# V by class and the dilated partial sums go through DRAM; one swap of the K halves for both sample granules

## Chip, cores and metric

One core of one Trainium2 chip runs the kernel. The metric is device time in microseconds (us), the median over executions; lower is better. The engines are PE (matrix products; PEld is its weight load), DVE and ACT (element-wise and row work), POOL (the same, slower), and SP, which in this kernel does nothing but issue every DMA, in one queue, in the order of the program.

## The reference, cut to what matters

Two encoder layers run over a prompt of 512 rows and a sample of 1024 rows, model width 1024. Layer 0 has grouped-query attention and differential attention, layer 1 has a dilated one, with 16 heads of 64. Only layer 1 is touched by two of the three edits:

```python
C_PATTERNS = ((128, 1), (512, 4), (2048, 16))       # (window, dilation)
def odd_layer(x, norm_g, w_in, w_out, c_q_norm, c_k_norm):
    z = rms_norm(x, norm_g) @ w_in
    q, k, v, gate = jnp.split(z, _split_points(ODD_SPLITS), axis=-1)
    q = partial_rope(rms_norm(q.reshape(B, S, C_HEADS, HEAD_DIM), c_q_norm))
    k = partial_rope(rms_norm(k.reshape(B, S, C_HEADS, HEAD_DIM), c_k_norm))
    o = dilated_attention(q, k, v).reshape(B, S, C_W)
    return x + (o * jax.nn.silu(gate)) @ w_out
def dilated_attention(q, k, v):                      # for each pattern: attention within a
    for window, dilation in C_PATTERNS:              # band, over the rows of one class
        o, lse = dilated_branch(q, k, v, window, dilation)   # (row modulo the dilation)
    w = jax.nn.softmax(jnp.stack(lses, axis=0), axis=0)      # the three are merged by their
    return jnp.sum(w[..., None] * jnp.stack(outs, axis=0), axis=0)   # softmax denominators
```

## The kernel before

**Tiling.** The rows are three granules of 512: granule 0 is the prompt, 1 and 2 are the halves of the sample. Each layer is cut into eight units; in layer 1 (kind "C") a unit is two heads, 128 columns. For each unit and granule there is a projection of K and V, one of Q and the gate, and the attention; at a layer's end come the output projection and the residual.

**K and q.** `qk_stages` normalises and rotates K or q into `st`, which a DMA transpose turns (L594: `K<-st`, `q<-st`). K is needed with its two halves of 64 partitions also the other way round: two DMAs, L599 and L600 (`K<-K`, 64 partitions each), make that swapped copy, for each of the three granules.

**V and the classes of four.** V is in `u.V`, 128 rows by 128-row tile. Pattern 1 uses it as it is. Patterns 2 and 3 are computed together ("p23") over rows of one class modulo four, and need V as `Vc`, where partition p holds rows 4p to 4p+3. Before the change `Vc<-V` (L682) copies each 128-row tile from SBUF to SBUF in a DMA of its own: four per granule.

**An attention batch** is a chain over four engines and a DMA: PE makes the scores `S` (L1122 for p23, L1170 and L1175 for pattern 1), DVE masks and takes the row maximum (L1097), ACT makes the exponential (L1107), ACT rounds to f16 (`h`, L796), DVE subtracts to get the low half (`h`, L800), SP issues a DMA transpose (`t<-h`, L359), and PE multiplies by V ("AV", L784).

**The send.** The p23 sums lie by class; pattern 1's lie by row. ACT packs the p23 sums and denominators into `pk`, and four DMAs (`pn<-pk`, L1152) bring them to row order in `pn`. The merge of the patterns reads `pn`, and its result `sg` is spilled to DRAM (`mixbuf<-sg`, L816). At the end of the layer it comes back (`f<-mixbuf`, L1269), is split and transposed, and goes through the output projection on PE (L492, operands `whl` and `t`).

**What sets the order.** Every piece is a stage with assumed costs (`dve()`, `act()`, `pe()`, and for a DMA an issue on SP plus a time and a tail) that a list-scheduling planner places; instructions are emitted in the planned order. The order of each engine is thus fixed when the program is built, and an engine that waits holds all that stands behind it. The planner also keeps tokens for buffers (`pnt` for `pn`, `vct` for `Vc`). Weights are loaded in f32 (`f<-in_w`, L415), squared on ACT (L423) for their norms (L432, L433 and L435 on PE), and split in two f16 halves (L473, L478).

Of the kernel before, what the change touches and what calls it, by code (L numbers as in the profile page):

```python
# [10 lines left out]
F32 = mybir.dt.float32  # L11
F16 = mybir.dt.float16
# [21 lines left out]
GI = [[0], [1, 2]]  # L34
# [179 lines left out]
def trunk_kernel(ctx: ExitStack, tc: tile.TileContext, A: dict, outs: list):  # L214
# [299 lines left out]
        return r  # L514


    def qk_stages(zb, ztok, evs, e2, tabs, tdep, ti, kind, isq, dst, dst_acq, dst_use, swap, dst_dep=()):

        b = {}
        t1t, stt_ = Token("t1"), Token("st")  # L520
# [75 lines left out]
        s = P.tdma(1024, f_T, [s, dst_dep], dst_acq, tuple(x for x in dst_use if x not in dst_acq) + (stt_,))  # L596
        if swap is None:
            return [s]
        w1 = dma(ISSUE, 0.25, lambda: nc.sync.dma_start(out=swap()[0:64], in_=dst()[64:128]), [s], (), dst_use)  # L599
        w2 = dma(ISSUE, 0.25, lambda: nc.sync.dma_start(out=swap()[64:128], in_=dst()[0:64]), [s], (), dst_use)  # L600
        return [s, w1, w2]


    class Unit:
        def __init__(self):
            self.q, self.sg, self.q_ready, self.sg_ready = {}, {}, {}, {}
            self.qtok, self.sgtok = {}, {}
            self.k_ready, self.v_ready, self.vc_ready = {}, {}, {}
            self.att_done = {}
            self.Vc = [None, None]  # L610

    last_mm = [None]
    proj_mm = {}
# [10 lines left out]
    def kv_piece(u, gi):  # L624
        g, t0, row = GRAN[gi]
        zb = {}
        ztok = Token("z")
        evs, vls = [], []
        for hf in range(2):
            pt = Token("pj")  # L630
            pb = {}
            mms = []
            for j in range(2):
                tl = t0 + 2 * hf + j

# [12 lines left out]
                proj_mm[u.l, g] = m  # L648
                mms.append(m)

            def f_ev(hf=hf, pb=pb):
                if "z" not in zb:
                    zb["z"] = new(ztok)
                S_.activation(out=zb["z"][:, :, 2 * hf:2 * hf + 2, :].rearrange("p h t d -> p t h d"),
                              in_=pb["ps"][:, :, 0:128].rearrange("p t (h d) -> p t h d", h=2), func=AF.Copy)
            evs.append(add("ACT", act(256), f_ev, mms, (), [pt, ztok], pos=P.pos - PB))
            r = row // 128 + 2 * hf

            def f_vh(r=r, pb=pb):
                if not hasattr(u, "V"):  # L660
                    u.V = new(u.vtok)
                S_.activation(out=u.V[:, r:r + 2, 0, :], in_=pb["ps"][:, :, 128:256], func=AF.Copy, scale=2.0 ** -15)
            first = (gi, hf) == (0, 0)
            vh = add("ACT", act(256), f_vh, [mms, None if first else u.v_open], [u.vtok] if first else (),
                     [pt] if first else [pt, u.vtok], pos=P.pos - PB)
            if first:
                u.v_open = vh

            def f_vl(r=r, pb=pb):
                stt(out=u.V[:, r:r + 2, 1, :], in0=pb["ps"][:, :, 128:256], scalar=2.0 ** -15,  # L670
                    in1=u.V[:, r:r + 2, 0, :], op0=M, op1=SU)
            vl = add("DVE", dve(256), f_vl, [vh], (), [pt, u.vtok], pos=P.pos - PB)
            vls.append(vl)
            if u.kind == "C":
                for j in range(2):
                    tl = t0 + 2 * hf + j

                    def f_vc(tl=tl, r=r, j=j):
                        if u.Vc[g] is None:
                            u.Vc[g] = lpool[0].tile([128, g + 1, 4, 256], F16, tag=f"Vc{g + 1}{u.vct[g].slot}", name=f"Vc{g + 1}", bufs=1)  # L680
                        p0 = 32 * (tl % 4)
                        nc.sync.dma_start(out=u.Vc[g][p0:p0 + 32, tl // 4, :, :],  # L682
                                          in_=u.V[:, r + j, :, :].rearrange("p a f -> p (a f)"))
                    if tl == 0:
                        u.vc_open = add("NONE", 0.0, None, [vl, u.tdep], [u.vct[g]])
                    vc = dma(ISSUE, 0.25, f_vc, [vl, u.vc_open], (), [u.vct[g], u.vtok])
                    u.vc_ready.setdefault(g, []).append(vc)
        u.v_ready[gi] = vls
        def kdst():
            if not hasattr(u, "K"):  # L690
                u.K = new(u.ktok)
            return u.K[:, 0, gi]
        u.k_ready[gi] = qk_stages(zb, ztok, evs, lambda: u.kvw.e2, lambda: u.ktab, u.tdep, t0, u.kind, False,
                                  kdst, [u.ktok] if gi == 0 else (), [u.ktok], lambda: u.K[:, 1, gi],
                                  () if gi == 0 else u.k_ready[0][0])
        if gi == 2:
            w_done(u.kvw, mms)

    def qg_piece(u, gi):
# [57 lines left out]
        def qdst():  # L757
            if gi not in u.q:
# [1 line left out]
            return u.q[gi]  # L760
        ti = row // 128 if u.kind == "C" else t0
        u.q_ready[gi] = qk_stages(zb, ztok, evs, lambda: u.qgw.e2, lambda: u.qtab, u.tdep, ti, u.kind, True,
                                  qdst, (), [qt], None)
        if gi == 2:
            w_done(u.qgw, mms)

# [299 lines left out]
    def att_C(u, gi):  # L1066
# [46 lines left out]
        def p23(hs):  # L1113
            def build():
                blocks = [(h, c) for h in hs for c in range(4)]

                def mm(s):
                    for i, (h, c) in enumerate(blocks):
                        q = u.q[gi][:, h, :].rearrange("p (r c) -> p c r", c=4)[:, c, :]
                        for sk in range(2):  # L1120
                            k = u.K[:, sk, GI[g][0]:GI[g][-1] + 1, h, :].rearrange("p g (t c) -> p c g t", c=4)[:, c]
                            T.matmul(s[:, L * i:L * i + L], q, k, start=(sk == 0), stop=(sk == 1))  # L1122

                def mxs(x):
                    if "md" not in ob:
                        ob["md"] = small(16, "md", 4).rearrange("p (c f) -> p c f", c=4)
                    h, c = x
                    return ob["md"][:, :, h] if c is None else ob["md"][:, c, h:h + 1]

                def avf(t4):  # L1130
                    if "o23" not in ob:
                        ob["o23"] = new(ot23).rearrange("p a b -> p (a b)").rearrange("p (c h d) -> p c h d", c=4, h=2)
                    for i, (h, c) in enumerate(blocks):
                        av(ob["o23"][:, c, h, :], t4, i * L // 128, L // 128,
                           lambda k, b: u.Vc[g][:, k, c, 128 * b + 64 * h:128 * b + 64 * h + 64])
                batch(mm, len(blocks) * pe(2 * L, 2), blocks, L, lambda x: u.m23[g][:, t0 // 4, :], mxs,
                      lambda x: ob["md"][:, x[1], 2 + x[0]:3 + x[0]], avf, [u.vc_ready[g]], avs23, ot23)
            return build

        def send():  # L1140
            def f_ev():
                ob["pk"] = lpool[0].tile([128, 4, 132], F32, tag=f"pk{pkt.slot}", name="pk", bufs=1)
                S_.activation(out=ob["pk"][:, :, 128:132], in_=ob["md"], func=AF.Copy)
                S_.activation(out=ob["pk"][:, :, 0:128], in_=ob["o23"].rearrange("p c h d -> p c (h d)"), func=AF.Copy)
            s = add("ACT", act(512) + 0.12, f_ev, avs23[-1:], [pkt], [ot23])
            s = add("NONE", 0.0, None, [s], [pnt])
            ob["sent"] = []
            for j in range(4):
                def f(j=j):
                    if j == 0:  # L1150
                        ob["pn"] = lpool[0].tile([128, 4, 132], F32, tag=f"pn{pnt.slot}", name="pn", bufs=1)
                    nc.sync.dma_start(out=ob["pn"][:, j, :],  # L1152
                                      in_=ob["pk"][32 * j:32 * j + 32, :, :].rearrange("p c f -> p (c f)"))
                ob["sent"].append(dma(ISSUE, 0.25, f, [s], (), [pkt, pnt]))
            if gi == 0 or gi == 2:
                close(u.vct[g], avs23)

# [559 lines left out]
```

## Time and profile before

| what | value |
|---|---|
| median of 3 runs | 1854.68 us (1853.79 to 1855.3) |
| profiled execution: time, span | 1854.62 us, 1852.4 us |
| mean granted clock of PE | 0.959 of full speed |
| busy share of the span: PE, PEld, DVE, ACT, POOL | 90%, 75%, 72%, 65%, 38% |
| busy share of the 16 DMA engines, main queue | 73.4% |

The span is the traced part of the profiled execution; 2.2 us of its time lie around it. The busy share of an engine is over the whole span, and an engine that is 90% busy can still stand still in single places. The program opens with layer 0 (to about 800 us), opens layer 1 (to 1000 us), runs the units of layer 1 (to about 1665 us), and ends with the last unit's batches and the output projection.

### The profile page before, as it was taken

What the parts mean: (1) busy time and instruction counts of PE and PEld (TensorE: products, weight loads), DVE (VectorE), ACT (ScalarE), POOL (GpSimd) and SP (SyncE); (2) the same over time, 40 slices, a digit from 0 to 9 for tenths busy, and PEclk for the clock granted to TensorE, in tenths of its full rate; (3) what the DMA queues carried; (4) which work ended last, traced back from release to release, by engine and by line L of the source; (5) the groups of instructions that cost most, each with busy time, mean ns of one, the idle gap of its engine ahead of it and who ended that gap; (6) DMA issues with size and microseconds to landing.
All of it is one profiled execution on the core that took longest, in us unless ns stands there. A gap on an engine that the chain in (4) does not pass through costs nothing. (4 is left out here: it accounts for less than half of the span.)

```text
span 1852.4 us, 44798 instructions
## 1 busy us (share of the span) xinstructions
PE 1675.0 (90%) x17626; PEld 1398.4 (75%) x17626; DVE 1332.2 (72%) x2985; ACT 1212.8 (65%) x2593; POOL 695.5 (38%) x1204
## 2 busy tenths in 40 slices
PE   4898978989999999699898999999999999995898
PEld 3776756878887878378787887888788888774788
DVE  7788878767888778965635778677777777787332
ACT  6488978767777767853425676678676757777220
POOL 6523333333463445312212344354444444452200
PEclk9999999999999999799899999999999999996999
DMA  9989999795565445689975676676766757776983
GB/s 251 191 157 166 182 177 167 146 163 113 98 125 101 109 92 122 147 198 224 207 176 128 122 150 131 138 143 140 147 132 144 137 116 151 148 145 140 232 230 103
DMA packets 788724, 282.06 MB, mean 152 GB/s; under 512 B 647072, under 2 KB 772256, under 8 KB 788512
## 3 DMA queue, kind: packets, MB, share of 16 engines
q1 hardware_dynamic: 788512, 279.19, 73.4%
q8 instruction: 138, 2.26, 0.5%
q14 instruction: 74, 0.61, 0.1%
HBM read 73.92 MB, written 25.17 MB: 53 GB/s over the span
## 5 line engine op out<-in xcount | busy, mean ns | idle before, releaser
L492 PE MATMUL pj<-whl,hT 128*128 128x256 f16 x7680 | 882.3, 275 | 22.2 <-DMA hT<-h 21.2
L492 PEld LDWEIGHTS <-hT 128*128 128x128 f16 x7968 | 782.8, 99 | 145.6 <-DMA hT<-h 23.1
L784 PEld LDWEIGHTS <-t 128*128 128x128 f16 x4992 | 200.5, 100 | 93.8 <-DMA t<-h 85.8
L1107 ACT ACTIVATE f<-f,cs,csc 128x256 f32<-128x256 f32 (+1 forms) x384 | 218.4, 570 | 65.5 <-DVE cs L778 65.4
L492 PEld LDWEIGHTS <-t 128*128 128x128 f16 x2304 | 228.9, 100 | 40.0 <-DMA t<-h 9.8
L800 DVE TENSOR_TENSOR h<-f,h 128x1024 f16<-128x1024 f32 x148 | 187.7, 1273 | 57.4 <-ACT h L796 55.0
L784 PE MATMUL pj<-V,t 128*128 128x64 f16 (+1 forms) x4032 | 178.7, 204 | 51.2 <-DMA t<-h 47.8
L492 PE MATMUL pj<-whl,t 128*128 128x256 f16 x1728 | 202.4, 279 | 8.2 <-DMA t<-h 8.2
L772 PE MATMUL S<-K,q 128*128 128x512 f16 x640 | 169.6, 399 | 33.3 <-ACT f L1024 19.1
L796 ACT ACTIVATE h<-f 128x1024 f16<-128x1024 f32 x168 | 175.5, 1051 | 21.9 <-DMA t<-h 19.8
L535 POOL TENSOR_SCALAR qs<-qs,we 128x8 f32<-128x8 f32 x87 | 44.5, 511 | 354.0 <-DVE qs L529 343.1
L261 POOL TENSOR_TENSOR qs<-qs,mhalf 128x8 f32<-128x8 f32 x87 | 147.8, 1699 | 7.3
L772 PEld LDWEIGHTS <-q 128*128 128x128 f16 x640 | 61.0, 101 | 91.7 <-issue 42.8
L854 DVE TENSOR_REDUCE as<-S 128x1 f32<-128x1024 f32 (+1 forms) x80 | 95.9, 1219 | 29.1 <-PE S L772 28.9
L423 ACT ACTIVATE t<-f 128x1024 bf16<-128x1024 f32 x74 | 77.8, 1051 | 44.5 <-DMA f<-in_w_in_dram 32.6
L864 ACT ACTIVATE f<-S,as,asc 128x1024 f32<-128x1024 f32 (+1 forms) x96 | 101.7, 1061 | 4.0 <-DVE h L800 0.5
L478 DVE SCALAR_TENSOR_TENSOR whl<-f,wsm,whl 128x1024 f16<-128x1024 f32 x68 | 87.7, 1305 | 8.2 <-ACT whl L473 8.2
L1332 DVE SCALAR_TENSOR_TENSOR f<-pj,os,f 128x256 f32<-128x256 f32 x96 | 41.9, 479 | 68.0 <-PE pj L492 61.2
L1018 DVE TENSOR_REDUCE bs<-S 128x1 f32<-128x1024 f32 x64 | 77.2, 1217 | 16.2 <-PE S L772 16.2
L800 POOL TENSOR_TENSOR h<-f,h 128x1024 f16<-128x1024 f32 x20 | 43.5, 2175 | 120.9 <-ACT h L796 120.9
L473 ACT ACTIVATE whl<-f,wsm 128x1024 f16<-128x1024 f32 x68 | 75.8, 1140 | 16.8 <-PE pj L492 14.3
L1122 PE MATMUL S<-K,q 128*128 128x256 f16 (+1 forms) x384 | 79.3, 371 | 4.6 <-DVE m L1097 4.6
(250 smaller groups left out, 2684.5 us busy)
## 6 DMA issues: line engine op xcount, KB each, us to landing
f<-in_w_in_dram SPq DMA_DIRECT2D x58, 512.0 KB, 5.3
mixbuf<-sg SPq DMA_DIRECT2D x48, 256.0 KB, 2.8
f<-mixbuf SPq DMA_DIRECT2D x24, 512.0 KB, 5.7
K<-K SPq DMA_DIRECT2D x78, 128.0 KB, 2.5
f<-in_w_out_dram SPq DMA_DIRECT2D x16, 512.0 KB, 4.5
pn<-pk SPq DMA_DIRECT2D x96, 66.0 KB, 2.2
x1buf<-f SPq DMA_DIRECT2D x12, 512.0 KB, 4.1
Vc<-V SPq DMA_DIRECT2D x96, 64.0 KB, 2.3
```

The lines of the kernel that those rows point to most:

```text
L261: G.tensor_tensor(y, v, mhalf[:, 0:n], ALU.pow)
L423: S_.activation(out=junk1(t1t), in_=b[i].rearrange("p k n -> p (k n)"), func=AF.Square, accum_out=b["s"][:, i:i + 1])
L478: stt(out=part(k, 1, i), in0=b[i][:, nk * k:nk * k + nk, :], scalar=sc(), in1=part(k, 0, i), op0=M, op1=SU)
L492: T.matmul(ps, lhs(k, a), wt(k, b), start=(k == 0 and i == 0), stop=(k == 7 and i == 2))
L772: T.matmul(out[:, 512 * i:512 * i + 512], q, u.K[:, st, gi, hk, :], start=(st == 0), stop=(st == 1))
L784: T.matmul(o, t4[:, 8 * a + base + k, :], v(k, b), start=(k == 0 and i == 0), stop=(k == nk - 1 and i == 2))
L796: S_.activation(out=b["hl"][:, 0, :], in_=b["e"], func=AF.Copy)
L800: (G if on_pool else V).tensor_tensor(b["hl"][:, 1, :], b["e"], b["hl"][:, 0, :], SU)
L854: V.tensor_reduce(out=b["s"][:, 0:nh], in_=b["S"].rearrange("p (h k) -> p h k", h=nh), op=ALU.max, axis=AX.X)
L864: S_.activation(out=b["e"][:, w * i:w * i + w], in_=b["S"][:, w * i:w * i + w], func=AF.Exp, bias=b["s"][:, 2 + i:3 + i], scale=u.sc, accu ...
L1107: S_.activation(out=b["e"][:, w * i:w * i + w], in_=b["e"][:, w * i:w * i + w], func=AF.Exp, bias=b["s"][:, i:i + 1], scale=u.sc, accum_ou ...
L1122: T.matmul(s[:, L * i:L * i + L], q, k, start=(sk == 0), stop=(sk == 1))
```

## The change

Three edits, and the costs that the planner assumes for the DMAs concerned:

- V goes to a DRAM tile `vd` in one DMA per granule of 256 KB (L676) and comes back from there as `Vc` in one of 256 KB (L683). `Vc` is now a tile per granule instead of one per group.
- `pk` goes to a DRAM tile `pd` in one DMA of 264 KB (L1158), and comes back in row order as `pn` in another (L1163).
- The K halves are swapped once for the prompt, and once for both sample granules after the second one's transpose (L700), in both layers. Granule 1 issues no swap of its own.

```diff
@@ qk_stages
         if swap is None:
             return [s]
-        w1 = dma(ISSUE, 0.25, lambda: nc.sync.dma_start(out=swap()[0:64], in_=dst()[64:128]), [s], (), dst_use)
-        w2 = dma(ISSUE, 0.25, lambda: nc.sync.dma_start(out=swap()[64:128], in_=dst()[0:64]), [s], (), dst_use)
-        return [s, w1, w2]
+        return [s] + swap(s)
@@ kv_piece
-            if u.kind == "C":
-                for j in range(2):
-                    tl = t0 + 2 * hf + j
...
-                        p0 = 32 * (tl % 4)
-                        nc.sync.dma_start(out=u.Vc[g][p0:p0 + 32, tl // 4, :, :],
-                                          in_=u.V[:, r + j, :, :].rearrange("p a f -> p (a f)"))
...
-                    vc = dma(ISSUE, 0.25, f_vc, [vl, u.vc_open], (), [u.vct[g], u.vtok])
-                    u.vc_ready.setdefault(g, []).append(vc)
+        if u.kind == "C":
...
+            vd = dr.tile([512, 256], F16, name=f"vd{box['n']}")
+            vs = dma(ISSUE, 0.5, lambda: nc.sync.dma_start(
+                out=vd.rearrange("(t p) f -> p t f", p=128),
+                in_=u.V[:, row // 128:row // 128 + 4].rearrange("p t a f -> p t (a f)")), [vls], (), [u.vtok])
...
+                nc.sync.dma_start(out=u.Vc[gi], in_=vd.rearrange("(p c) f -> p c f", c=4))
...
+            vc = dma(ISSUE, 0.5, f_vc, [vs, u.vc_open], (), [u.vct[g]])
+            u.vc_ready.setdefault(g, []).append(vc)
...
+        def swap(s):
...
+            for a, b in ((0, 64), (64, 0)):
+                def f_w(a=a, b=b):
+                    x = slice(GI[g][0], GI[g][-1] + 1)
+                    nc.sync.dma_start(out=u.K[a:a + 64, 1, x], in_=u.K[b:b + 64, 0, x])
+                r.append(dma(ISSUE, 0.25 + 0.2 * g, f_w, [s, u.k_ready.get(1)], (), [u.ktok]))
+            return r
         u.k_ready[gi] = qk_stages(zb, ztok, evs, lambda: u.kvw.e2, lambda: u.ktab, u.tdep, t0, u.kind, False,
-                                  kdst, [u.ktok] if gi == 0 else (), [u.ktok], lambda: u.K[:, 1, gi],
+                                  kdst, [u.ktok] if gi == 0 else (), [u.ktok], swap if gi != 1 else None,
@@ send
-            s = add("NONE", 0.0, None, [s], [pnt])
-            ob["sent"] = []
-            for j in range(4):
...
-                    nc.sync.dma_start(out=ob["pn"][:, j, :],
-                                      in_=ob["pk"][32 * j:32 * j + 32, :, :].rearrange("p c f -> p (c f)"))
-                ob["sent"].append(dma(ISSUE, 0.25, f, [s], (), [pkt, pnt]))
+            pd = dr.tile([512, 132], F32, name=f"pd{box['n']}")
+            s = dma(ISSUE, 0.5, lambda: nc.sync.dma_start(out=pd.rearrange("(p c) f -> p c f", c=4), in_=ob["pk"]),
+                    [s], (), [pkt])
...
+                nc.sync.dma_start(out=ob["pn"], in_=pd.rearrange("(j p) f -> p j f", p=128))
+            ob["sent"] = [dma(ISSUE, 0.6, f, [s], [pnt])]
```

The changed costs and stages also move the order. The programs' SP queues differ from layer 0 on, PE's order from the end of layer 0. All later lines of the file stand ten lines further down (L784 is L794, L816 is L826, L1122 is L1132, L1269 is L1279). No instruction of PE, DVE, ACT or POOL is added or removed.

The first place is SP's queue in an ordinary unit of layer 1, before (the numbers behind a tile's name count tiles):

```order
L816 DMA mixbuf_72<-sg_15020 128x4x128
L359 DMA_TRANSPOSE t_16778<-h_16745 128x16x128
L359 DMA_TRANSPOSE t_16820<-h_16780 128x16x128
L682 DMA Vc_16887<-V_15813 32x4x256 x4
L594 DMA_TRANSPOSE q_16942<-st_16817 128x8x128
L1152 DMA pn<-pk 128x1x132 x4
L682 DMA Vc_16887<-V_15813 32x4x256 x4
L359 DMA_TRANSPOSE t_17063<-h_16986 128x16x128
L594 DMA_TRANSPOSE K_16068<-st_17052 128x8x128
```

The same place of the changed program:

```order
L359 DMA_TRANSPOSE t_16793<-h_16754 128x16x128
L594 DMA_TRANSPOSE q_16826<-st_16795 128x8x128
L359 DMA_TRANSPOSE t_16831<-h_16797 128x16x128
L683 DMA Vc_16874<-vd_96 128x1024
L826 DMA mixbuf_72<-sg_15020 128x4x128
L676 DMA vd_98<-V_15825 128x4x256
L1158 DMA pd_97<-pk 128x528
L683 DMA Vc_16979<-vd_98 128x1024
L1163 DMA pn<-pd_97 128x4x132
L359 DMA_TRANSPOSE t_17068<-h_16996 128x16x128
L594 DMA_TRANSPOSE K_16082<-st_17057 128x8x128
```

Twelve plain DMAs stood between two `t` transposes; now six stand there, of which two read what another one has just written, with one DMA between the write and the read (`vd_98`, `pd_97`).

The second place is SP's queue at the end of the units, in the last unit, before:

```order
L359 DMA_TRANSPOSE t_24868<-h_24808 128x16x128
L682 DMA Vc_24928<-V_23414 32x4x256 x8
L816 DMA mixbuf_72<-sg_23462 128x4x128
L1152 DMA pn<-pk 128x1x132 x4
L359 DMA_TRANSPOSE t_25002<-h_24902 128x16x128
L594 DMA_TRANSPOSE q_25014<-st_24988 128x8x128
```

The same place of the changed program:

```order
L359 DMA_TRANSPOSE t_24821<-h_24749 128x16x128
L683 DMA Vc_24879<-vd_127 128x1024
L683 DMA Vc_24885<-vd_129 128x1024
L594 DMA_TRANSPOSE q_24891<-st_24811 128x8x128
L1158 DMA pd_130<-pk 128x528
L826 DMA mixbuf_72<-sg_23450 128x4x128
L1163 DMA pn<-pd_130 128x4x132
L359 DMA_TRANSPOSE t_24945<-h_24922 128x16x128
```

Thirteen plain DMAs and a `t` stood ahead of this q; now two stand there, and the q is ahead of the send.

The third place is PE's order there, one row for each group of matmuls. Before:

```order
L784 MATMUL pj_24941<-V_21971,t_25002 128x64
...
L1122 MATMUL S_25054<-K_23553,q_25014 128x256
...
L1122 MATMUL S_25159<-K_23553,q_25097 128x256
...
L1122 MATMUL S_25188<-K_23553,q_25097 128x256
...
L784 MATMUL pj_25205<-Vc_24928,t_25174 128x64
...
L784 MATMUL pj_25205<-Vc_24928,t_25243 128x64
...
L492 MATMUL pj_25324<-whl_24002,t_25268 128x256
```

And of the changed program:

```order
L1132 MATMUL S_24926<-K_23489,q_24891 128x256
...
L794 MATMUL pj_24895<-V_21949,t_24945 128x64
...
L794 MATMUL pj_25104<-Vc_24879,t_25074 128x64
...
L794 MATMUL pj_25104<-Vc_24879,t_25091 128x64
...
L1132 MATMUL S_25164<-K_23489,q_25130 128x256
...
L1132 MATMUL S_25183<-K_23489,q_25130 128x256
...
L794 MATMUL pj_25350<-Vc_24879,t_25323 128x64
```

Before, the scores of the last granule (`S_25159`, `S_25188`) stood ahead of the AV of the granule before it (`t_25174`); now they stand behind both AV of that granule (`t_25074`, `t_25091`), and the last granule's AV (`t_25323`) stands ahead of the output projection.

## Rows read from the trace of the kernel before

**Rows 1.** Head of the page: busy us (share) xinstructions, each engine; the main DMA queue.
```profile
PE 1675.0 (90%) x17626; PEld 1398.4 (75%) x17626; DVE 1332.2 (72%) x2985; ACT 1212.8 (65%) x2593; POOL 695.5 (38%) x1204
...
q1 hardware_dynamic: 788512, 279.19, 73.4%
```

**Rows 2.** Windows: length, then busy us of PE, PEld, DVE, ACT, POOL; clock, DMA share, GB/s.
```profile
1000.00:1600.00 600.00, 575.09 (x6500) 496.15 (x6498) 443.98 (x1346) 414.11 (x1064) 258.88 (x454) 0.99 0.68 135
...
1665.00:1705.00 40.00, 19.70 (x176) 13.56 (x172) 31.11 (x110) 28.68 (x70) 10.49 (x18) 0.62 0.68 145
1705.00:1853.00 148.00, 135.60 (x1295) 119.14 (x1293) 50.42 (x128) 32.85 (x55) 12.80 (x22) 0.96 0.73 183
```

**Rows 3.** PE's waits, 1000 to 1600 us: waiter, releaser, us in total, times, longest.
```profile
PE pj L784 <- DMA t<-h: 13.8, 16, 3.2
```

**Rows 4.** The SP queue's waits, whole span.
```profile
SPq L359 <- DVE h L800: 179.5, 63, 11.4
...
SPq L599 <- DMA K<-st: 41.6, 19, 3.4
```

**Rows 5.** SP's timeline in an ordinary unit: start, us in issue, line, DMA, count.
```profile
1273.64 3.13 SPq L682 DMA_DIRECT2D Vc<-V  x4
1276.88 0.53 SPq L816 DMA_DIRECT2D mixbuf<-sg  x1
1277.52 3.65 SPq L1152 DMA_DIRECT2D pn<-pk  x4
1281.21 2.56 SPq L682 DMA_DIRECT2D Vc<-V  x4
```

**Rows 6.** DMAs by kind: count, KB each, median us from issue to landing.
```profile
mixbuf<-sg SPq DMA_DIRECT2D x48, 256.0 KB, 2.8
...
K<-K SPq DMA_DIRECT2D x78, 128.0 KB, 2.5
pn<-pk SPq DMA_DIRECT2D x96, 66.0 KB, 2.2
...
Vc<-V SPq DMA_DIRECT2D x96, 64.0 KB, 2.3
...
f<-x1buf SPq DMA_DIRECT2D x4, 256.0 KB, 4.6
```

**Rows 7.** SP's timeline, end of the units.
```profile
1662.41 5.16 SPq L682 DMA_DIRECT2D Vc<-V  x8
...
1668.31 2.57 SPq L1152 DMA_DIRECT2D pn<-pk  x4
1670.98 2.64 SPq L359 DMA_TRANSPOSE t<-h  x1
1673.72 1.25 SPq L594 DMA_TRANSPOSE q<-st  x1
```

**Rows 8.** PE's timeline there: start, us, matmuls; in brackets idle before, and its releaser.
```profile
1664.84 0.86 PE L784 MATMUL pj<-V,t 128*128 128x64 f16 x24
...
1670.64 0.58 PE L433 MATMUL pj<-wsm,ones 128*128 128x1 f32 x2 [4.74 <-ACT t L423]
1675.64 1.46 PE L784 MATMUL pj<-V,t 128*128 128x64 f16 x24 [4.41 <-DMA t<-h]
1676.91 3.85 PE L1122 MATMUL S<-K,q 128*128 128x256 f16 x16
...
1691.95 1.46 PE L784 MATMUL pj<-Vc,t 128*128 128x64 f16 x24
...
1699.70 1.46 PE L784 MATMUL pj<-Vc,t 128*128 128x64 f16 x24 [0.85 <-DMA t<-h]
...
1704.51 1.89 PE L492 MATMUL pj<-whl,t 128*128 128x256 f16 x8 [1.64 <-DMA t<-h]
```

**Rows 9.** DVE's timeline there: what this q's transpose and the last `t` read.
```profile
1662.37 1.22 DVE L800 TENSOR_TENSOR h<-f,h 128x1024 f16<-128x1024 f32 x1
...
1668.72 0.68 DVE L590 TENSOR_TENSOR st<-t,st 128x512 f16<-128x512 f32 x1
```

More of the change, by code (lines that the diff above doesn't have):

```diff
@@ L514, in h_deps, with qk_stages @@
         return r
-    def qk_stages(zb, ztok, evs, e2, tabs, tdep, ti, kind, isq, dst, dst_acq, dst_use, swap, dst_dep=()):
+    def qk_stages(zb, ztok, evs, e2, tabs, tdep, ti, kind, isq, dst, dst_acq, dst_use, swap=None, dst_dep=()):
         b = {}
@@ L609, in __init__ @@
             self.att_done = {}
-            self.Vc = [None, None]
+            self.Vc = {}
     last_mm = [None]
@@ L673, in kv_piece, with f_vc @@
             vls.append(vl)
-            if u.kind == "C":
-                for j in range(2):
-                    tl = t0 + 2 * hf + j
-                    def f_vc(tl=tl, r=r, j=j):
-                        if u.Vc[g] is None:
-                            u.Vc[g] = lpool[0].tile([128, g + 1, 4, 256], F16, tag=f"Vc{g + 1}{u.vct[g].slot}", name=f"Vc{g + 1}", bufs=1)
-                        p0 = 32 * (tl % 4)
-                        nc.sync.dma_start(out=u.Vc[g][p0:p0 + 32, tl // 4, :, :],
-                                          in_=u.V[:, r + j, :, :].rearrange("p a f -> p (a f)"))
-                    if tl == 0:
-                        u.vc_open = add("NONE", 0.0, None, [vl, u.tdep], [u.vct[g]])
-                    vc = dma(ISSUE, 0.25, f_vc, [vl, u.vc_open], (), [u.vct[g], u.vtok])
-                    u.vc_ready.setdefault(g, []).append(vc)
+        if u.kind == "C":
+            box["n"] = box.get("n", 0) + 1
+            vd = dr.tile([512, 256], F16, name=f"vd{box['n']}")
+            vs = dma(ISSUE, 0.5, lambda: nc.sync.dma_start(
+                out=vd.rearrange("(t p) f -> p t f", p=128),
+                in_=u.V[:, row // 128:row // 128 + 4].rearrange("p t a f -> p t (a f)")), [vls], (), [u.vtok])
+            def f_vc():
+                x = f"Vc{gi}"
+                u.Vc[gi] = lpool[0].tile([128, 4, 256], F16, tag=x, name=x, bufs=1)
+                nc.sync.dma_start(out=u.Vc[gi], in_=vd.rearrange("(p c) f -> p c f", c=4))
+            if t0 == 0:
+                u.vc_open = add("NONE", 0.0, None, [vls, u.tdep], [u.vct[g]])
+            vc = dma(ISSUE, 0.5, f_vc, [vs, u.vc_open], (), [u.vct[g]])
+            u.vc_ready.setdefault(g, []).append(vc)
         u.v_ready[gi] = vls
@@ L692, in kdst @@
             return u.K[:, 0, gi]
+        def swap(s):
+            r = []
+            for a, b in ((0, 64), (64, 0)):
[4 more added lines that the diff above has]
+            return r
         u.k_ready[gi] = qk_stages(zb, ztok, evs, lambda: u.kvw.e2, lambda: u.ktab, u.tdep, t0, u.kind, False,
-                                  kdst, [u.ktok] if gi == 0 else (), [u.ktok], lambda: u.K[:, 1, gi],
+                                  kdst, [u.ktok] if gi == 0 else (), [u.ktok], swap if gi != 1 else None,
                                   () if gi == 0 else u.k_ready[0][0])
@@ L762, in qg_piece @@
         u.q_ready[gi] = qk_stages(zb, ztok, evs, lambda: u.qgw.e2, lambda: u.qtab, u.tdep, ti, u.kind, True,
-                                  qdst, (), [qt], None)
+                                  qdst, (), [qt])
         if gi == 2:
@@ L1134, in avf @@
                         av(ob["o23"][:, c, h, :], t4, i * L // 128, L // 128,
-                           lambda k, b: u.Vc[g][:, k, c, 128 * b + 64 * h:128 * b + 64 * h + 64])
+                           lambda k, b: u.Vc[g + k][:, c, 128 * b + 64 * h:128 * b + 64 * h + 64])
                 batch(mm, len(blocks) * pe(2 * L, 2), blocks, L, lambda x: u.m23[g][:, t0 // 4, :], mxs,
@@ L1145, in send, with f @@
             s = add("ACT", act(512) + 0.12, f_ev, avs23[-1:], [pkt], [ot23])
-            s = add("NONE", 0.0, None, [s], [pnt])
-            ob["sent"] = []
-            for j in range(4):
-                def f(j=j):
-                    if j == 0:
-                        ob["pn"] = lpool[0].tile([128, 4, 132], F32, tag=f"pn{pnt.slot}", name="pn", bufs=1)
-                    nc.sync.dma_start(out=ob["pn"][:, j, :],
-                                      in_=ob["pk"][32 * j:32 * j + 32, :, :].rearrange("p c f -> p (c f)"))
-                ob["sent"].append(dma(ISSUE, 0.25, f, [s], (), [pkt, pnt]))
+            box["n"] = box.get("n", 0) + 1
+            pd = dr.tile([512, 132], F32, name=f"pd{box['n']}")
+            s = dma(ISSUE, 0.5, lambda: nc.sync.dma_start(out=pd.rearrange("(p c) f -> p c f", c=4), in_=ob["pk"]),
+                    [s], (), [pkt])
+            def f():
+                ob["pn"] = lpool[0].tile([128, 4, 132], F32, tag=f"pn{pnt.slot}", name="pn", bufs=1)
+                nc.sync.dma_start(out=ob["pn"], in_=pd.rearrange("(j p) f -> p j f", p=128))
+            ob["sent"] = [dma(ISSUE, 0.6, f, [s], [pnt])]
             if gi == 0 or gi == 2:
```

## Prediction

> **What bounds the kernel now.** I read the head of the page first. PE is busy for 1675.0 of 1852.4 us, so 177 us is all that is to be had without taking work from PE, and the change takes none. DVE and ACT, at 72% and 65%, are no bound over the whole [rows 1]. A table by windows then shows where PE stands still. In the units of layer 1, from 1000 to 1600 us, it is idle for 600 - 575.1 = 24.9 us at a granted clock of 0.99. In the 40 us in which the units end it is idle for 20.3 us at 0.62, that is, with stretches at the lower level of 1.2 GHz, and in the last 148 us for 12.4 [rows 2]. So the units are nearly full and their end is half empty.
>
> PE's waits in the units say what the 24.9 us are: 13.8 of them are the AV product waiting for the transposed probabilities `t`, at 16 places, none longer than 3.2 us [rows 3]. `t` is a DMA in SP's queue, and so the queue matters. The queue itself mostly waits for the computation: 179.5 us for the low half `h`, and only 41.6 us, in 19 waits, for a K transpose to land before its swap [rows 4]. What the edits shorten are the bursts of plain DMAs: in an ordinary unit four `Vc`, a spill, four `pn` and four more `Vc` keep the queue for 10 us, from 1273.64 to 1283.77 [rows 5].
>
> **The change, part by part.**
>
> *Issues removed.* `Vc` and `pn` go from 96 DMAs each to 48 (24 writes and 24 reads), `K<-K` from 78 to 52 [rows 6]: 48 + 48 + 26 = 122 DMAs fewer. An issue takes 5.16 / 8 = 0.65 us for `Vc`, 2.57 / 4 = 0.64 for `pn` [rows 7], and 0.53 for a single spill [rows 5]. At 0.63 that is 77 us of queue time.
>
> *Waits added.* Each read must wait on SP until its write has landed, and everything behind stands still too, the `t` above all. The trace has no such write. The nearest row is the spill, `mixbuf<-sg`: the same 256 KB, SBUF to DRAM, 2.8 us. The same-sized load from DRAM, `f<-x1buf`, takes 4.6; the small SBUF copies take 2.2 and 2.3 [rows 6]. I take 2.8, since size and direction agree, and keep 2.2 and 4.6 as bounds. With nothing between the write and the read the queue stands for 2.8 - 0.6 = 2.2 us, with one DMA between for 1.6. Going through the changed order I count 28 of 48 reads with a hold, 46 us in all. In the other 20 so much stands between that the write has landed.
>
> *K swaps.* A third of the waits for a K transpose goes, since granule 1 has no swap of its own: by the same count 41.6 us become about 24.5. SP's queue in all: -77 + 46 - 17 = -48 us.
>
> *What this is worth in the units.* Queue time is hidden unless a `t` stands behind it and PE has run out of other work. That is the 13.8 us. Of a hold of 10 us, as in rows 5, about 4 are left in the same place (two `Vc` reads, a write each, the `pn` read, one hold), so I take -5 of the 13.8, something over a third. All of it, -13.8, is the far end. Against this stands more traffic: V and the partial sums are moved twice, 24 x (256 + 264 KB) = 12.8 MB more. The main queue's 279.19 MB took 73.4% of the span, 1360 us of all 16 engines [rows 1], or 4.9 us per MB: 62 us over some 800 us of layer 1, a share of 0.76 where it was 0.68 [rows 2]. A `t` lands later by some tenths; at the 16 places where PE waits for one, and some more that have no slack now, I take +2, with 0 and +8 as ends. Units: **-3** (-10 to +8).
>
> *The end of the units.* The last unit's first q is ready at 1668.72 + 0.68 = 1669.40 [rows 9], but its transpose is issued at 1673.72, behind eight `Vc`, a spill, four `pn` and a `t` [rows 7]; PE begins its scores at 1676.91, after two waits of 4.74 and 4.41 us [rows 8]. In the new order two reads stand before this q, and those scores can begin 4.3 us earlier, at 1672.6. The wait for the weight norm (4.74) and the AV that waited 4.41 then stand behind the scores, in time that is empty anyway. But the order also takes cover away. From a first score to its AV, 1676.91 to 1691.95, 15.0 us pass [rows 8]. Before, the scores of the last granule filled part of them; now they stand behind both AV, and have 15.0 us of their own before the output projection. Worked through: the first AV at 1672.6 + 15.0 = 1687.6, two AV of 1.5 to 1690.6, the last scores, and their AV 15.0 later at 1705.6; the projection begins at 1707.1, where it was 1704.51: +2.6. On the other side three AV batches now stand ahead of the projection that stood behind its beginning, 3 x 0.86 = 2.6 at the higher clock, as the AV at 1664.84 [rows 8], and the 1.64 wait is gone. Sum: **-2**. If the second AV is 7.75 us behind the first, as at 1699.70 [rows 8], it is +6; if the 4.3 us come through whole, -7.
>
> *Layer 0 and its other edges.* Only the merged swap is there, two DMAs and up to one wait less per unit, beside PE work that hides them except where scores wait for K. If that cover is gone the sample's first batch waits for both halves of K. I take **-1** (-3 to +3).
>
> Sum: -3 - 2 - 1 = -6 us on the profiled execution's 1854.62, which is the median but for 0.06: **1848.6 us**.
>
> **A rule against it.** The row says that 256 KB to DRAM land 0.3 us later than 128 KB within SBUF [rows 6]. The Trainium skill, "DMA: Bandwidth & Descriptors", section "Anatomy of one DMA", says that most of a DMA's fixed 2 us is the receipt from the target memory, with HBM the heaviest, and that this delay can be surprisingly long there; its section on latency gives HBM 0.2 us on average and 2 us at high load. With 2 us more on each of 48 reads, as an estimate from that page, the holds would be 142 us and SP would lose 48 us where by the row it gains 48. No run here shows yet which holds.
>
> **The rivals.**
>
> *Nothing comes of it (1852 to 1857).* For it: most of SP's waiting is for DVE, ACT and PE, so a queue that is free earlier waits earlier; PE's 13.8 us are spread over 16 small waits, and the end's gain and loss cancel in my own sum to 2 us. Against it: the bursts of rows 5 and 7 stand before a `t` that was ready.
>
> *Slower, by the read after the write.* The place is the SP queue behind each `vd` and `pd` write, where a `t` stands next. Holds beyond 77 + 17 = 94 us turn the queue's gain into a loss; that is reached when a write lands in 2.8 + 48 / 48 = 3.8 us in place of 2.8, less than the 4.6 of the load. At 4.6 the holds are 46 + 48 x 1.8 = 132, the queue loses 38, the waits for `t` grow by some 5 us where I took off 5, traffic takes its 2, and the end loses some 2 of its own, its last `t` standing behind such a read: 1854.6 + 5 + 2 + 2 - 1 = 1863. The rule above is this rival's mechanism. Against it: 2.8 is the median of 48 spills amid the same traffic.
>
> *A larger gain.* All the waits for `t` go and the 4.3 us come through: 1854.6 - 10 - 7 - 1 = 1837. Against it: the order at the end leaves 15 us uncovered twice.
>
> **How the numbers follow.** Measurement can tell about 0.2%, 3.7 us, from no change. The forecast's case, 1840 to 1851, gets 0.47, the larger gain 0.05, no change 0.25, slower 0.23. Faster by over 0.2% (below 1851) is 0.52, within 0.25, slower 0.23. The terms' ends, taken as independent, give -9 and +14 around the forecast: 1840 to 1862, which leaves about the larger gain and half of the worst cases outside.
>
> **What would show it.** Right: `vd` and `pd` writes landing in about 2.8 us; SP waiting for them about 46 us in all and for K some 25; PE's wait for `t` from 1000 to 1600 below 10 us; the last unit's first scores some 4 us earlier, and then two stalls of over 5 us ahead of the output projection. Wrong: writes that land later than 3.8 us, PE's waits for `t` grown, or the output projection starting more than 6 us later against the units' end. What I can least see is the new order, which has moved every batch of layer 1 by some places; a batch whose room on PE is less than its chain costs more than any term above.

## The result, and the profile after

The changed kernel takes 1837.74 us (median of 4 runs, 1834.61 to 1838.94) where the kernel before took 1854.51: a ratio of 0.9918, with a 95% interval of 0.9897 to 0.9939. A second measurement on another chip gave 0.9925 (0.9905 to 0.9945). The direction was forecast. The size, 16.8 us where 6 were forecast, is outside the range.

The head of the page and the main queue, of the changed kernel [rows 1]:

```profile
PE 1666.3 (91%) x17626; PEld 1398.9 (76%) x17626; DVE 1329.1 (72%) x2985; ACT 1213.1 (66%) x2593; POOL 688.5 (37%) x1204
...
q1 hardware_dynamic: 791040, 291.97, 76.2%
```

The same window of the units as before [rows 2], then the two stretches around the end of the units:

```profile
1000.00:1600.00 600.00, 586.37 (x6704) 509.77 (x6702) 449.10 (x1364) 428.60 (x1093) 263.00 (x468) 0.99 0.75 155
...
1650.00:1692.00 42.00, 27.39 (x292) 20.55 (x290) 33.50 (x102) 29.12 (x71) 14.30 (x25) 0.75 0.82 178
1692.00:1837.00 145.00, 133.08 (x1248) 117.83 (x1248) 52.24 (x135) 35.88 (x64) 11.47 (x16) 0.96 0.74 186
```

PE's idle time from 1000 to 1600 us falls from 24.9 to 13.6 us, and 6704 matmuls fit in where 6500 did. All of PE's waits there, in the changed kernel [rows 3]:

```profile
PE pj L794 <- DMA t<-h: 12.7, 15, 1.6
PE pj L794 <- DVE wsm L442: 0.9, 1, 0.9
```

The wait for `t`, on which the prediction was built, has hardly moved: 13.8 to 12.7 us. What has gone are six waits of the kernel before that the prediction did not price. They stand below the first row of that view, and add up to 11.0 us:

```profile
PE S L1175 <- DVE md L1097: 2.9, 3, 1.9
PE pj L435 <- ACT t L423: 2.3, 1, 2.3
PE pj L784 <- DVE V L670: 2.1, 2, 1.8
PE pj L784 <- DVE cf L1224: 1.6, 1, 1.6
PE pj L784 <- DVE wiz L446: 1.1, 1, 1.1
PE pj L435 <- DVE sg L749: 1.0, 1, 1.0
```

To see where the time came from I compared when PE reaches the same share of its work (matmul columns, added up from the trace's PE instructions). From 54% to 90% of the columns lie the units of layer 1; this stretch, called "units" below, takes 616.2 us before and 598.4 after: **-17.8 us**. The rest is +4.4 (layer 0), +1.1 (its end and the opening of layer 1) and -3.0 (the last 10%). Layer 0 takes 681.8 to 690.5 us in the fourteen runs below that swap K as before and are the same there, so its +4.4 shows nothing. Of the 17.8 us, 12.4 are idle time in the stretch. The other 5.4 are a shorter busy time for the same matmuls; some 3 of them go with the granted clock, at whose lower level PE was busy for 16.1 us of the stretch before and for 10.2 after, and the remaining 2 are not explained. Before, behind 3 us of waiting that ended at 1308.89 and 1310.01 us, the window reads

```profile
1300.00:1320.00 20.00, 16.96 (x169) 12.93 (x168) 19.31 (x56) 12.63 (x32) 9.24 (x16) 0.83 0.89 188
```

a granted clock of 0.83, that is, part of it at 1.2 GHz.

The DMAs of the changed kernel by kind [rows 6], and the SP queue's waits [rows 4]:

```profile
mixbuf<-sg SPq DMA_DIRECT2D x48, 256.0 KB, 3.1
...
K<-K SPq DMA_DIRECT2D x26, 256.0 KB, 4.3
pd<-pk SPq DMA_DIRECT2D x24, 264.0 KB, 3.2
pn<-pd SPq DMA_DIRECT2D x24, 264.0 KB, 3.3
...
vd<-V SPq DMA_DIRECT2D x24, 256.0 KB, 4.0
Vc<-vd SPq DMA_DIRECT2D x24, 256.0 KB, 2.9
...
t<-h SPq DMA_TRANSPOSE x232, 4.6
```

```profile
SPq L359 <- DVE h L810: 187.0, 68, 10.3
...
SPq L683 <- DMA vd<-V: 33.3, 15, 3.7
...
SPq L1163 <- DMA pd<-pk: 18.4, 13, 3.3
SPq L700 <- DMA K<-st: 17.5, 13, 2.6
```

The 28 holds that were counted are there, 51.7 us for the 46 forecast, though the write of V lands in 4.0 us and not in 2.8. `t` does not land later (4.6 us, before 4.8). The end of the units, PE's timeline [rows 8]:

```profile
1657.60 0.86 PE L794 MATMUL pj<-V,t 128*128 128x64 f16 x24
1660.16 3.85 PE L1132 MATMUL S<-K,q 128*128 128x256 f16 x16 [1.70 <-DMA q<-st]
...
1674.87 1.46 PE L794 MATMUL pj<-Vc,t 128*128 128x64 f16 x24 [7.48 <-DMA t<-h]
...
1694.90 1.46 PE L794 MATMUL pj<-Vc,t 128*128 128x64 f16 x24 [3.87 <-DMA t<-h]
1697.81 2.53 PE L492 MATMUL pj<-whl,t 128*128 128x256 f16 x11 [1.45 <-DMA t<-h]
```

The first q is early, and by more than was worked out: from the start of the AV to that of the scores it takes 2.6 us where it took 12.1 [rows 8], 9.5 less where 4.3 were forecast. The cover is gone, with stalls of 7.5 and 3.9 us, of which only the first is the stall of over 5 us that was forecast; and from that AV to the output projection it takes 40.2 us where it took 39.7.

### The profile page after: what moved, and what is told of

The parts are those of the page before. It is cut to its first block, busy times and chain, and to the rows that moved or that the text cites. A ratio compares the mean times of both kernels' runs of the same rounds, so it can differ in the third digit from the quotient of the medians.

```text
span 1836.9 us, 44593 instructions
## 1 busy us (share of the span) xinstructions
PE 1666.3 (91%) x17626; PEld 1398.9 (76%) x17626; DVE 1329.1 (72%) x2985; ACT 1213.1 (66%) x2593; POOL 688.5 (37%) x1204
## 4 chain that ended last, share of the span: by engine, by line
PE 36%; DMA 7%; DVE 3%; ACT 2%; issue 1%; POOL 1%; SPq 0%; DVEq 0%
PE pj L492 26%; DMA t<-h 6%; PE pj L794 3%; PE S L1132 3%; PE pj L506 2%; PE S L1180 1%; DVE f L1107 1%; DMA x1buf<-f 1%; ACT f L1117 1%; PE S L1185 0%; DVE h L810 0%; ACT t L423 0%; DMA q<-st 0%; DVE f L1342 0%; DMA pn<-pd 0%
## 5 line engine op out<-in xcount | busy, mean ns | idle before, releaser
L794 PEld LDWEIGHTS <-t 128*128 128x128 f16 x4992 | 205.4, 102 | 106.3 <-DMA t<-h 96.1
L794 PE MATMUL pj<-V,t 128*128 128x64 f16 (+1 forms) x4032 | 181.6, 205 | 54.1 <-DMA t<-h 52.8
L535 POOL TENSOR_SCALAR qs<-qs,we 128x8 f32<-128x8 f32 x87 | 39.5, 454 | 344.5 <-DVE qs L529 331.0
L864 DVE TENSOR_REDUCE as<-S 128x1 f32<-128x1024 f32 (+1 forms) x80 | 95.9, 1219 | 30.3 <-PE S L782 30.1
L759 DVE SCALAR_TENSOR_TENSOR sg<-sg,pj 128x256 f32<-128x256 f32 x96 | 39.5, 416 | 69.6 <-ACT sg L753 68.6
L1132 PE MATMUL S<-K,q 128*128 128x256 f16 (+1 forms) x384 | 79.3, 371 | 1.7 <-DMA q<-st 1.7
```

The costliest lines, as they stand in the source:

```text
L794: T.matmul(o, t4[:, 8 * a + base + k, :], v(k, b), start=(k == 0 and i == 0), stop=(k == nk - 1 and i == 2))
L864: V.tensor_reduce(out=b["s"][:, 0:nh], in_=b["S"].rearrange("p (h k) -> p h k", h=nh), op=ALU.max, axis=AX.X)
```

## The experiments

Each ratio is to the kernel before on the same chip, with its 95% interval. The columns "units" and "matmuls" are of one profiled execution of each run, and those differ: executions of e18 alone go from 1839.47 to 1856.17 us, and layer 0, in which PE's order is the same in all runs, scatters by 8.7 us. The units were taken twice for the changed kernel only, 598.4 and 598.6. The profiled executions of e1, e4, e9 and e18 lie 5 to 10 us below their medians. So a few us in the column "units" prove nothing by themselves; the ratios do. "Repeat" is worked out from a program's order alone: for each of layer 1's batches, the PE work that stands between its scores and its AV (columns at 0.11 us per 256), and then the share of batches for which this agrees to 0.2 us with the batch eleven places, that is one unit, later. The column comes out about so without the pairs at layer 1's two ends; over all 77 pairs it is lower (0.32 before, 0.62 changed, 0.52 in e14, 0.49 in e17, 0.21 in e18), in nearly the same order of runs.

```
run                           ratio    interval         units us  matmuls     repeat
                                                                  1000-1600
before                        1                         616.2     6500        0.43
changed                       0.9918   0.9897-0.9939    598.4     6704        0.82
e1  its order, old DMAs       0.9966   0.9949-0.9982    598.8     6669        0.82
e2  old order, new DMAs       1.0179   1.0152-1.0206    637.1     6318        0.43
e3  K swap only               1.0067   1.0043-1.0092    622.0     6454        0.43
e4  V and pn only             0.9879   0.9852-0.9906    591.7     6764        0.82
e5  changed again             0.9925   0.9905-0.9945    598.6     6701        0.82
e6  e4's order, old DMAs      0.9915   0.9891-0.9939    597.9     6701        0.82
e7  light plan                1.0097   1.0075-1.0119    624.6     6442        0.32
e8  heavy plan                0.9940   0.9917-0.9964    600.3     6696        0.06
e9  V only                    0.9868   0.9846-0.9889    591.5     6765        0.86
e10 pn only                   1.0024   1.0008-1.0041    611.1     6576        0.55
e11 late plan                 1.0016   1.0001-1.0030    620.7     6455        0.57
e12 light and late plan       0.9953   0.9936-0.9969    608.6     6589        0.46
e13 V, write gated            0.9894   0.9875-0.9913    595.1     6736        0.66
e14 copies after all tiles    1.0063   1.0039-1.0087    620.7     6469        0.69
e15 V, heavy plan             0.9913   0.9893-0.9932    605.9     6626        0.32
e16 V, K merged in place      0.9886   0.9866-0.9906    595.0     6732        0.86
e17 copies planned as 0.6     0.9921   0.9896-0.9946    600.0     6689        0.66
e18 copies planned as 1.2     0.9974   0.9955-0.9994    608.2     6593        0.30
```

**Order or DMAs (e1, e2, e6).** e1 keeps every engine's order of the changed kernel and puts the old copies where the reads stand; e6 does the same to e4. e2 keeps the order of before and issues write and read back to back.

```diff
 e1, e6
-            vs = dma(ISSUE, 0.5, lambda: nc.sync.dma_start(out=vd..., in_=u.V...), [vls], (), [u.vtok])
+            vs = dma(ISSUE, 0.5, None, [vls], (), [u.vtok])
-                nc.sync.dma_start(out=u.Vc[gi], in_=vd.rearrange("(p c) f -> p c f", c=4))
+                for j in range(4):
+                    nc.sync.dma_start(out=u.Vc[gi][32 * j:32 * j + 32, :, :], in_=u.V[:, row // 128 + j, :, :]...)
 e2, in the fourth of the four copies' stages; the other three issue nothing
+                        nc.sync.dma_start(out=vd..., in_=u.V[:, row // 128:row // 128 + 4]...)
+                        nc.sync.dma_start(out=u.Vc[g][:, tl // 4, :, :], in_=vd...)
```

e1: 

> Every engine's order is that of the changed kernel, but V and the partial sums go by the four small SBUF copies of before, issued where the changed kernel issues its read; nothing is issued in the place of the write. The merged K swap stays. Theory O (the gain comes from the order that the planner makes once it sees 1.2 us of queue in place of 2.4): most of the 16.8 us stay, 1836 to 1844, and PE's waits for DVE and ACT between 1000 and 1600 us stay below 2 us as in the changed kernel. Theory D (the gain is the queue's own time: fewer issues in front of the transposes): the queue is as full as before, so 1850 to 1860, and PE's wait for the transposed probabilities rises from 12.7 to 20 us or more.

e2: 

> Every engine's order is that of before, but in place of four Vc copies one write to DRAM and one read stand at the fourth copy's place, and the same for the partial sums, with nothing between write and read. K is swapped as before. The queue saves 96 issues of 0.63 us (60 us) and waits 48 times for a write of 3.2 to 4.0 us less its issue, 2.6 to 3.4 each (125 to 163 us). Theory O: no gain, 1854 to 1864. Theory D in the form that the number of DMAs counts: below 1848.

e6: 

> The order of the run without the merged K swap (which took 0.988 of before), with the four small copies for V and for the partial sums in place of write and read. In the units of layer 1 the first such exchange left the time as it was (598.8 us where the changed kernel took 598.4). Theory O: as there, 0.988 to 0.992. Theory D: the DRAM form itself is worth half or more of the gain, 0.994 to 1.000.

e1's units take 598.8 us in its profiled execution, as in the changed kernel, with 15.5 us of PE's waits for `t` and 1.1 for all else: by this reading the gain in the units is the order's. The whole run lies between the two theories, 0.9966: of the changed kernel's 0.8% the order alone keeps 0.34, and the other 0.4 to 0.5 need the DMAs as well. After the units e1 takes 205.9 us where the changed kernel takes 200.8, some 5 of the 8 us or so that are missing; where the others lie is not shown. In e4's order the old copies cost 6.2 us in the units (597.9 in e6, 591.7 in e4) and 0.36% of the whole, with intervals that overlap. So the order alone gives 0.34% in e1 and 0.85% in e6, and with these orders the DMAs add some 0.4%, clear of noise in the first pair only. e2, SP's waits:

```profile
SPq L688 <- DMA vd<-V: 70.0, 24, 5.8
SPq L1161 <- DMA pd<-pk: 54.6, 22, 4.1
```

124.6 us of holds, and PE's wait for `t` from 1000 to 1600 us is 30.3 us. This is the rival that a read behind its write costs more than it saves, and in the order of before it is true: +1.8%. The changed kernel, whose plan puts other issues between, has 28 such holds of 51.7 us. So neither the order nor the DMAs explain the gain alone: with the old copies the new order gives 0.34%, with the old order the new DMAs lose 1.8%, and together they gain 0.8%.

**Part by part (e3, e4, e9, e10).** Each undoes the other parts and is planned anew.

e3: 

> Only the merged swap of K, planned anew; V and the partial sums as before. In the changed kernel layer 0, which has this edit alone, ends 5 us later than before. If the merged swap costs that, the time here is 1855 to 1862, with the 5 us there by the end of layer 0. If the loss is the order's chance, the layer 1 units, which also lose a swap, give it back: 1848 to 1855.

e4: 

> V and the partial sums through DRAM as in the changed kernel, planned anew, K swapped per granule as before. Layer 0 is then exactly that of before. If the merged swap cost 5 us in layer 0 and gives nothing in layer 1: 1830 to 1834. If the merged swap is a part of the gain in layer 1 (two issues and a wait fewer per unit): 1838 to 1848.

e9: 

> V alone through DRAM, planned anew; partial sums and K as before. Theory O (the gain in the units comes from the plan, which places the pattern 2 and 3 batches by the time at which Vc and pn are said to be there): a part of the gain, 0.990 to 0.998. Theory L (a new plan is a draw of luck): anything from 0.990 to 1.010, with no relation to the sum of this and the next run.

e10: 

> The partial sums alone through DRAM, planned anew. Theory O: the other part, 0.990 to 0.998, and this times the run with V alone near the 0.988 of both. Theory L: as for V alone.

V alone makes more than the whole gain, 0.9868; the partial sums lose 0.2%, and theory O, which gave each a part of the gain, misses both. The merged swap loses 0.7% alone and 0.4% on top of e4. It does not lose it in layer 0, as the expectations of e3 and e4 had it: e3 takes 0.6 us more there than before, so that e4's hit on 1830 to 1834 is luck in part. PE's order in the units is the same in e3 as in the kernel before, and in the changed kernel as in e4, and there the runs with the merged swap take 5.8 and 6.7 us more, one execution each. e16 leaves every other instruction where it stood:

```diff
+                    if gi == 1:
+                        return
-                    x = slice(gi, gi + 1)
+                    x = slice(GI[g][0], GI[g][-1] + 1)
```

e16: 

> V alone through DRAM in its own order, with the K swaps of the sample's first half left out at their place and both halves swapped at the place of the second, 256 KB each. Every other instruction stands where it stood. If the merged swap's loss of 0.4 to 0.7% comes from the later and larger DMA: 0.990 to 0.994. If it comes from the orders that the planner made of it: 0.984 to 0.988.

Units +3.5 us against e9; the ratio, 0.9886, lies between the two cases, and its interval overlaps e9's. The 256 KB swap lands in 4.4 us where e9's 128 KB one takes 3.0. Which wait passes that on to PE is not settled: the `t` that stand behind a swap are too few to show it.

**The planner's numbers alone (e7, e8, e11, e12).** These are the kernel before with its own DMAs; only what the planner is told of the `Vc` and `pn` copies differs.

```diff
-dma(ISSUE, 0.25, f_vc, ...)      dma(ISSUE, 0.25, f, [s], (), [pkt, pnt])
+dma(0.3, 0.25, ...)              # e7; 0.9 in e8
+dma(ISSUE, 0.25, ..., tail=3.6)  # e11; with 0.3 in e12
```

e7: 

> The kernel before with its own DMAs, but the planner is told 0.3 us of queue for each Vc and pn copy in place of 0.6. No DMA is changed. Theory O in its strict form (a plan with less queue time packs the batches better, and the queue keeps up): 0.985 to 0.993. Theory L (any new plan is a draw of luck of some 0.5% either way): between 0.995 and 1.007. Theory D: the plan is wrong by 1.2 us at each burst, so slower, over 1.002.

e8: 

> The opposite: 0.9 us of queue for each Vc and pn copy in the plan, the DMAs as before. Theory O: the plan spreads the bursts further and the time grows, 1.003 to 1.015. Theory L: between 0.993 and 1.007 with no relation to the light plan.

e11: 

> The kernel before with its own DMAs and its 0.6 us of queue each in the plan, but the plan is told that Vc and pn come 2.35 us later (6.2 us from the first issue of a burst to the data, where it was told 3.9; the changed kernel's plan has 4.8, the heavy plan 5.1, the light one 2.7). Theory S (a plan that expects these data later than it did gives the real queue room): 0.990 to 0.997, units of layer 1 near 600 us where before took 616. Theory Q (what counts is the queue time in the plan): as before, 0.998 to 1.004. Theory L: no relation, could be slower.

e12: 

> The light plan (0.3 us of queue for each copy), which took 1.010 of before and 624.6 us in the units, with the later arrival as in the run before this: 5.05 us from the first issue to the data. Theory S: units near 600 us, 0.990 to 0.997. Theory Q: the light plan's loss stays, 1.006 or more. Theory L: no relation.

The same DMAs take from 0.994 to 1.010 of the time by the order alone. Theory O as stated falls (the light plan is slower, the heavy one faster), and theory S falls with e11. e12 has the time that S gave (0.9953), but 608.6 us in the units and not near 600: the later arrival helps the light plan and not the plan of before, which is theory L, no relation. e5 is the changed kernel again, beside e6 to e8. 

> The changed kernel itself, beside the next three on one chip. 0.990 to 0.994 of before, as measured first.

**What in the V edit gives the order (e13, e14, e15, e17, e18).**

```diff
 e13
-            vs = dma(ISSUE, 0.5, ..., [vls], (), [u.vtok])
+            vs = dma(ISSUE, 0.5, ..., [vls, u.vc_open], (), [u.vtok, u.vct[g]])
 e14, the copies of before, moved behind the loop over the tiles
-                    vc = dma(ISSUE, 0.25, f_vc, [vl, u.vc_open], (), [u.vct[g], u.vtok])
+                vc = dma(ISSUE, 0.25, f_vc, [vls, u.vc_open], (), [u.vct[g], u.vtok])
 e15
-vs = dma(ISSUE, ...)       vc = dma(ISSUE, 0.5, f_vc, ...)
+vs = dma(2 * ISSUE, ...)   vc = dma(2 * ISSUE, 0.5, f_vc, ...)
 e17, e18: the four copies of before in one stage
+            vc = dma(0.6, 0.5, f_vc, [vls, u.vc_open], (), [u.vct[g], u.vtok])    # 1.2, 0.25 in e18
```

e13: 

> V alone through DRAM (0.987 of before, 591.5 us in the units of layer 1), but the write to DRAM waits for the Vc buffer to be free, as the copies of before did; the DMAs are the same. Theory B (the gain comes from the write being free of the Vc buffer, so that only one read per granule, not all the copying, stands between the last use of Vc and the next): most of the gain goes, units over 608 us, 0.996 to 1.006. Theory G (the gain comes from one DMA that waits for all four tiles in place of copies tile by tile) and theory Q (fewer issues in plan and queue): the units stay below 600 us, 0.985 to 0.991.

e14: 

> The kernel before with its four copies and its costs in the plan, but no copy is issued until all four tiles of V are there. Theory G: units below 604 us, 0.988 to 0.995. Theories B and Q: no gain, 0.997 to 1.008.

e15: 

> V alone through DRAM, but the planner is told 1.2 us of queue for the write and for the read, 2.4 together as for the four copies of before. The DMAs are the same. Theory Q: the gain goes with the queue time in the plan, units over 606 us, over 0.994. Theories B and G: it stays, units below 600 us, 0.985 to 0.992.

e17: 

> No DRAM, no merged swap: V by the four small SBUF copies of before, partial sums and K as before. Only the plan differs: the four copies are one stage, after all four tiles, which the planner counts as 0.6 us of queue (they take about 2.6). Worked out from the plans alone: PE's order then repeats from unit to unit as in all the kernels that took under 600 us in the units; with 1.2 us in the next run it does not. Theory P (the gain is that repeating plan, which comes when the planner sees one short stage for Vc): units below 603 us, 0.989 to 0.995, from the kernel's own old DMAs. Theory D' (the plan needs the short DMAs it assumes): the queue falls behind, 1.000 or more.

e18: 

> The same code with 1.2 us in the plan for the one stage, nearer to what the copies take. Its order does not repeat. Theory P: units over 606 us, 0.997 to 1.010. If it is as fast as the run before it, the repeating order is not the cause.

B falls with e13 (3.6 us of the 24.7 lost), G with e14. e15 loses 14.4 of the 24.7 us in the units, less than Q asked in the whole. e17 and e18 bring neither V nor the partial sums through DRAM, and differ in two numbers of one call, the queue time (0.6 and 1.2) and the time behind it (0.5 and 0.25). Both came as theory P had them, and e17, with nothing but the old DMAs, makes the changed kernel's gain: 0.9921. In e13 PE's order in the units is that of e17; with V through DRAM it takes 595.1 us there for 600.0 and 0.9894 of before, the intervals overlapping. The window of the units, first of e17, then of e18:

```profile
1000.00:1600.00 600.00, 583.86 (x6689) 506.67 (x6689) 448.92 (x1359) 422.75 (x1084) 262.15 (x468) 0.99 0.71 138
```

```profile
1000.00:1600.00 600.00, 576.82 (x6593) 498.81 (x6592) 448.52 (x1360) 419.89 (x1077) 265.44 (x458) 0.99 0.70 137
```

Idle time of PE: 16.1 us against 23.2. All of PE's waits in these windows, first of e17, then of e18:

```profile
PE pj L794 <- DMA t<-h: 15.2, 16, 2.4
PE pj L794 <- DVE wsm L442: 0.9, 1, 0.9
```

```profile
PE pj L794 <- DMA t<-h: 23.1, 22, 2.7
```

So in this pair the whole difference is in the waits for `t`, while e18 has none of the other kinds: an order moves waits from one kind to another, and only their sum tells. Of DVE's waits from 1000 to 1600 us, the kernel before and then e9:

```profile
DVE sg L749 <- ACT sg L743: 34.3, 16, 4.6
DVE h L800 <- ACT h L796: 27.4, 31, 3.0
DVE V L670 <- ACT V L662: 20.8, 9, 5.8
...
DVE f L1097 <- PE S L1170: 17.4, 8, 4.7
```

```profile
DVE h L810 <- ACT h L806: 47.7, 49, 3.1
DVE sg L759 <- ACT sg L753: 42.1, 21, 4.2
...
DVE f L1107 <- PE S L1180: 4.1, 4, 3.0
```

In e9 DVE waits more behind ACT's half of the same `h`, and no longer for up to 5.8 us in front of V (1.3 at most) or 4.7 us before scores; its waits for `sg`, up to 4.2 us, remain. Whether this is what helps PE was not tested: in e8, whose units take 600.3 us, DVE waits 17.9 us for `h` and 12.3 in front of V.

## Why the prediction was wrong

*What bounds the kernel* held, but for the clock: PE, with a rest of 177 us that its waits can give. Its busy time itself fell from 1675.0 to 1666.3 us, with the same matmuls.

*Issues removed, waits added, K's waits* held in sum. The holds are 51.7 us for 46, K's 17.5 for 25. The 2.8 us taken for a write were too low for V (4.0) and near for the partial sums (3.2). So one sign of being wrong, writes later than 3.8 us, came for V, and the time fell all the same.

*The units, -3 us*: this is the step that failed. "I take -5 of the 13.8" priced one kind of wait, the one that SP can cause, in an order that I took as given. That kind moved by 1.1 us, from 13.8 to 12.7, and the +2 for a later `t` is not seen either. What fell are the other waits in the same view, from 11.0 to 0.9 us, and with them some 3 us of lower clock; all the units gave 17.8 us, outside the term's -10 to +8. The new order is the main part of it: with the old copies put back the units of e1 and e6 still take 17.4 and 18.3 us less than before (the same as the changed kernel's, and 6.2 us more than e4's), and the small copies of before, counted as one stage of 0.6 us, get to 600.0 us and 0.9921 with no DRAM for them (e17). It is not all of it: over the whole run the order alone keeps 0.34% of the 0.8 (e1). The prediction named the new order as what it could least see, and gave it no term; six kernels with the same kind of DMAs for V show that it ranged from -16 to +8 us in the units (e8, e12, e11, e14, e7 and e18 against 616.2).

*The end of the units, -2 us*: right in kind in both halves, the early q and the lost cover, with other sizes (9.5 us earlier for 4.3, one stall of over 5 us for two). The last 10% of PE's work took 3.0 us less; that this is near -2 is in part luck, since the sizes that were off cancel.

*Layer 0, -1 us*: not told apart from its scatter. The merged swap costs time over the whole run (e3, 1.0067), and in the units by one execution each; the prediction had it at nothing there beyond queue time.

*The larger gain, 1837*, has the right number with the wrong mechanism: the waits for `t` did not go. *Nothing comes of it* is refuted by the interval. *Slower, by the read after the write* is a true mechanism whose condition the order did not fulfil: 51.7 us of holds, below the 94 at which the queue would lose, where e2 has 124.6. The Trainium skill's rule that the receipt is heaviest for HBM ("DMA: Bandwidth & Descriptors", "Anatomy of one DMA") is not settled by these rows. That section describes DMAs issued from gpsimd, and here SP issues them; a landing time holds the moving of the data and the receipt together. 256 to 264 KB written to DRAM landed in 3.1 to 4.0 us, 256 KB within SBUF, over 64 partitions, in 4.3. The holds worked out from its latency section, 142 us, were 51.7.

Left open: what in an order makes it good. That the plan's numbers alone make 0.5% of the time is shown by e17 against e18. That the repeating of the order is the cause is not shown: e8 is as quick (600.3) with an order that does not repeat, and e14, whose order repeats more than e17's (0.69 for 0.66), takes 620.7. The version that beats both kernels is e9, V alone.

## What to carry to other kernels

Where a planner orders instructions by costs, an edit of a DMA changes two things, the DMA and the plan; put the old operation into the new order and the new one into the old order before you credit either. Price every releaser in the bounding engine's list of waits and compare their sum, not only the one that the edit seems to touch. Here a copy through DRAM paid where something else stood between the write and the read in the queue, and lost 1.8% where nothing did; and parts of a change are to be timed one by one: here one part makes 1.3% and the two others give back 0.5%.

## What the runs showed of the hardware

256 KB from SBUF to DRAM landed in 2.8 us for one source (`mixbuf<-sg` before) and in 3.0 (e15) to 4.3 us (e4) for another, `vd<-V`. A swap of 256 KB within SBUF over 64 partitions took 4.3 us in the changed kernel, where one of 128 KB took 3.0 beside it and 2.5 in the kernel before. And with nothing between write and read, 46 holds cost the queue 124.6 us, 2.7 us each.
